# A two-layer hybrid decoder trunk: HGRN2 decay levels in pairs, rounded inner norms and full-width transposes

## The chip, the cores and the metric

The kernel runs on one core of one Trainium2 chip. The metric is the device time of one execution in microseconds. The engines are named as in the profile: PE (TensorE's products), PEld (TensorE's weight loads), DVE (VectorE), ACT (ScalarE), POOL (GpSimd) and SP (SyncE, which here issues weight loads from memory).

## The reference

One inference step of two layers, for a prompt of 256 tokens and 8 samples of 4 tokens each, with the same weights. The model is 1024 wide. A layer is

```
u    = RMSNorm(x)                      # x: 288 tokens x 1024
cols = u @ W_in                        # one projection, split among four mixers and four gate blocks
o_A  = RG-LRU(cols)    o_B = RWKV-7(cols)    o_C = HGRN2(cols)    o_D = dilated attention(cols)
x   += W_o( sum_n sigmoid(G_n) * (o_n @ P_n) )
v    = RMSNorm(x)
x   += W_down( gelu(causal_dwconv3(v @ W_gate)) * (v @ W_up) )
```

and a last RMSNorm follows the second layer. Each mixer is 256 wide. HGRN2 (four heads, a state of 128 x 64 each), in chunks of tokens, is

```
bcum = cumsum(log f) ;  dec[t,s] = exp(bcum[t] - bcum[s]) for s <= t
att  = sum_k q[t,k] k[s,k] dec[t,s,k]
o    = (q * exp(bcum)) @ S + att @ v
S    = S * exp(bcum_last) + (k * exp(bcum_last - bcum))^T v
```

RWKV-7 (four heads of 64) updates a state by S = S w + (S a) b^T + v k^T and reads it with r; its output is normalised by head, given a bonus from r, k and v, and gated. The outputs are y for both groups and the new states of every mixer.

## The kernel before

Everything is kept with features on partitions and the N = 288 token columns (256 of the prompt, then 32 of the samples) along the free axis. A weight block of 128 x 1024 in 32 bits is loaded by SP; `chunk` (L320) splits it into a high half, rounded to fp32r by ACT (L185, tile `h`), and a low half, the rest, by DVE (L193, tile `l`). Three buffers of each exist (TAGS, L135). `prod` (L330) then makes three products per 128 x 128 block: high by high, high by low, low by high, each with 288 columns. The tiles `tp` hold the halves of the normalised x, `pm` and `xc` are accumulators. There are 7,200 such products in the program; we call them projections. Three helpers record every product, transpose and activation, so all of these carry one line each: `mm` L179, `tr` L182, `act` L185; `tt` (L193), `stt` (L196) and `ts` (L200, L202) record element-wise work on DVE, or on POOL where the engine is given as G.

A product whose inputs are plain 32-bit tiles is done unrounded and leaves two records in the trace; one of fp32r tiles leaves one. `exact` (L357) splits a tile into rounded halves first and makes two rounded products. `square_sum` (L363) is the RMS norm's sum: POOL squares and adds seven of the eight blocks of x, ACT squares the eighth, and two unrounded products with a matrix of ones sum over partitions into `xc`; then ACT takes logarithm and exponential, which gives the row scale `rs`. It is called four times, and the first norm has a form of its own (`first_norm`, L389).

The mixers are Python generators: A (RG-LRU), B (RWKV-7), S (B's samples), C twice (HGRN2, one pass for each pair of heads), D (attention), E (its samples). `unit` writes three blocks of a projection and then calls `mix`, which takes up to four of the generators one step further, each up to its next `yield`; GAP and ORDER (L140, L147) set the pace. A scheduler then sets every engine's own order at build time with a timeline of its own, so a changed step moves its neighbours too. The accumulator banks limit how far steps can run ahead: three `pm`, two `xb` (RWKV, attention), three `xc` (HGRN2, the projections without mixers).

In `branch_c`, after the gates and a running sum b of log f, the scores of a chunk of 64 tokens are made by levels. Level m (1, 2, 4, 8, 16, 32) looks at blocks of 2m tokens: POOL subtracts from b its value at the block's middle (`tt(G, ...)`), ACT takes the exponentials of both halves, DVE multiplies the first half by k and the second by q (tiles `c`), PE makes eight 64 x 64 products (`level_out`), and a masked copy (`copy_predicated`, L971) puts those entries of the result that the level owns into the score tile `att` (`kc`). The diagonal is a level of its own, with k and q as they are. For the samples, whose chunks are four tokens, the diagonal and levels 1 and 2 also make two 32 x 32 products each, copied into `zs` (L977). Later steps transpose v and the decayed k with `tr`, or with products by an identity for the sample part, and multiply the samples' old state (`s0`) by q in one 32-row product for each head.

In `branch_b`, `scores` makes the products of two of the tiles at, rt, bt, kt, head by head, for 128-token chunks; three masked score matrices `zz` come from (kt, at), (bt, rt) and (kt, rt). The inner norms (`bones`, `cent`: block matrices of ones) go by `exact` with temporaries of the tag `b`, of which there are 20.

Of the kernel before, what the change touches and what calls it, by code (L numbers as in the profile page):

```python
# [18 lines left out]
P = 128  # L19
# [3 lines left out]
NB = 8  # L23
# [29 lines left out]
for _n, _c in CONSTS:  # L53
# [3 lines left out]
         ("b1", 32), ("l2", 32), ("l4", 32), ("l8", 32), ("l16", 32), ("dg", 64), ("us", 128), ("ui", 128),  # L57
# [7 lines left out]
def _constants():  # L65
# [40 lines left out]
    for w in (1, 2, 4, 8, 16, 32):  # L106
        def half(a, b):
            return (a // (2 * w) == b // (2 * w)) & (a % (2 * w) < w) & (b % (2 * w) >= w)
        putm(f"u{w}", half(s, t))
# [4 lines left out]
    putm("dg", s == t)  # L114
# [9 lines left out]
    putm("sdg", s == t)  # L124
    return {"cst": c, "msk": m, **{k: v.astype(np.float32) for k, v in more.items()}}


def dkeys():
# [7 lines left out]
        "tmp": (1152, 4), "rs": (1152, 1), "a": (1280, 10), "b": (1152, 20), "kb": (2048, 10), "c2": (2688, 10), "kc": (2048, 7),  # L136
# [14 lines left out]
def trunk(ctx, tc, I, O):  # L151
# [68 lines left out]
    V.memset(ones, 1.0)  # L220
    few = cp.tile([P, 4], F32, name="few")
# [141 lines left out]
    def square_sum():  # L363
# [4 lines left out]
        for k in range(KT):  # L368
            q = T("tmp")
            if k < KT - 1:  # L370
                tt(G, q, x[:, k], x[:, k], MUL)
                if acc is not None:
                    tt(G, q, q, acc, ADD)
                acc = q
            else:
                act(q, x[:, k], AF.Square)
            if k >= KT - 2:
                mm(p, ones, q, start=k == KT - 2, stop=k == KT - 1)
        r = T("rs")
# [141 lines left out]
    def branch_b(l, cols, rs, ys_, spawn):  # L521
# [25 lines left out]
        at, rt, bt, kt, bv, elast = [], [], [], [], [], []  # L547
# [4 lines left out]
        for i in range(2):  # L552
# [10 lines left out]
            lw, ta = T("b"), T("b")  # L563
# [7 lines left out]
        for i in range(2):  # L571
            pn = X("xb")[:, :N]
            exact(pn, bones, pre[i][3], "b")
# [6 lines left out]
        for i in range(2):  # L580
# [6 lines left out]
            b = T("b")  # L587
            stt(b, ta, 1.0, kk, ADD, MUL)

            ep, em = T("b"), T("b")  # L590
# [28 lines left out]
            exact(pb, bones, rk, "b")  # L619
# [129 lines left out]
        for pair in (((0, bt, 0), (0, kt, 1)), ((0, v, 2), (1, v, 2)), ((1, bt, 0), (1, kt, 1))):  # L749
# [24 lines left out]
        for m in (2, 4, 8, 16):  # L774
# [7 lines left out]
            V.transpose(fl(Y4), fl(X4))  # L782

# [29 lines left out]
        zz = [[], []]  # L813
        for a, q, mk in ((kt, at, "us"), (bt, rt, "ui"), (kt, rt, "ui")):
            pair = scores(a, q)
            yield
            for h, p in enumerate(pair):
                z = R([P, 4, P], "kb")
                G.memset(z, 0.0)
                V.copy_predicated(z, Mn(mk, 4), p)  # L820
                zz[h].append(z)
# [64 lines left out]
        for i in range(2):  # L886
            p = X("xb")[:, :N]
            exact(p, cent, py[i], "b")
# [5 lines left out]
        for i in range(2):  # L894
            p = X("xb")[:, :N]
            exact(p, bones, sqs[i], "b")
# [15 lines left out]
    def branch_c(l, i, cols, rs, ys):  # L912
# [690 lines left out]
```

## The time and profile before

| | |
|---|---|
| median of 3 runs | 1209.07 us (1206.88 to 1209.87) |
| profiled execution | 1212.02 us |
| its span, first to last instruction | 1210.2 us |
| mean granted clock of TensorE | 0.990 |
| busy: PE / PEld / DVE / ACT / POOL | 97% / 91% / 70% / 51% / 46% |
| read from memory, written | 187.08 MB, 6.49 MB |

Busy shares are means over the whole span; stretches differ, so the tables by stretch and the timelines matter more. A granted clock of 1.00 is 2.4 GHz, 0.50 is 1.2 GHz. In a timeline the bracket behind a row gives the idle time in front of that instruction on its engine and what released it. Matmuls are pipelined, so on PE the distance from one start to the next is the price of a product, and not its length.

### The profile page before, as it was taken

The numbers are of one execution on the slowest core, as the hardware profiler recorded it, in microseconds if no ns is written. First come the engines' busy times: TensorE is split into PE (matmuls) and PEld (weight loads), VectorE is DVE, ScalarE is ACT, GpSimd is POOL, SyncE is SP. The second block draws the span as 40 slices with busy tenths as digits, with TensorE's granted clock in tenths as the row PEclk, the third lists the DMA queues.
The fourth block names the chain that finished last, engine by engine and source line by source line (L and its number), as shares of the span: only waits on it lengthen the run. The fifth ranks groups of instructions, "written<-read, shape, count | busy, mean of one in ns | idle before, by whom it ended". The sixth has DMA issues, their size and how long they took to land.

```text
span 1210.2 us, 26415 instructions
## 1 busy us (share of the span) xinstructions
PE 1172.3 (97%) x10564; PEld 1102.2 (91%) x10564; DVE 848.4 (70%) x1385; ACT 611.3 (51%) x1042; POOL 552.8 (46%) x864
## 2 busy tenths in 40 slices
PE   7998999999999999999998999999999999999997
PEld 6987788998999999999998977899889999999996
DVE  7898856566578888865568888566655878888543
ACT  5776447445355444443367844565444554444332
POOL 3744555250345665642238337524221736665322
PEclk9999999999999999999998999999999999999999
DMA  7444145357645555454543432643775445545552
GB/s 258 132 130 141 63 152 203 112 168 277 209 133 190 161 171 168 164 176 163 171 153 124 141 106 89 214 145 115 253 250 168 150 152 171 172 158 171 167 171 77
DMA packets 64043, 196.33 MB, mean 162 GB/s; under 512 B 8417, under 2 KB 12641, under 8 KB 63921
## 3 DMA queue, kind: packets, MB, share of 16 engines
q1 hardware_dynamic: 61872, 189.56, 47.4%
q0 software_dynamic: 1328, 4.33, 1.0%
q8 instruction: 83, 1.36, 0.5%
q10 hardware_dynamic: 720, 0.76, 0.2%
q14 instruction: 40, 0.32, 0.1%
HBM read 187.08 MB, written 6.49 MB: 160 GB/s over the span
## 4 chain that ended last, share of the span: by engine, by line
PE 74%; DVE 9%; POOL 6%; ACT 4%; DMA 4%; issue 3%; DVEq 0%; SPq 0%; ACTq 0%; POOLq 0%
PE pm L179 43%; PE xc L179 24%; PE xb L179 5%; DVE c L193 2%; DVE l L193 2%; POOL b L193 1%; ACT L185 1%; DMA c<-in_vc 1%; DMA w<-in_w 1%; DVE b L196 1%; POOL a L193 1%; ACT a L185 1%; ACT h L185 1%; PE xc L182 1%; DMA kc<-in_cs 1%
## 5 line engine op out<-in xcount | busy, mean ns | idle before, releaser
L179 PE MATMUL pm<-tp,h 128*128 128x288 f32 x2880 | 608.3, 302 | 3.8 <-ACT h L185 2.3
L185 ACT ACTIVATE h<-w 128x1024 fp32r<-128x1024 f32 x299 | 316.5, 1059 | 393.8 <-issue 182.1
L179 PEld LDWEIGHTS pm<-tp,h 128*128 128x128 f32 x2880 | 471.3, 191 | 17.7 <-issue 7.3
L193 DVE TENSOR_TENSOR l<-w,h 128x1024 fp32r<-128x1024 f32 x299 | 380.6, 1273 | 118.6 <-ACT h L185 117.6
L179 PE MATMUL pm<-tp,l 128*128 128x288 f32 x1440 | 430.4, 299 | 4.5 <-DVE l L193 4.5
L179 PEld LDWEIGHTS pm<-tp,l 128*128 128x128 f32 x1440 | 274.7, 191 | 7.1 <-DVE l L193 5.0
L179 PE MATMUL xc<-tp,h 128*128 128x288 f32 x896 | 183.9, 296 | 1.6 <-ACT tp L185 0.9
L179 PEld LDWEIGHTS xc<-tp,h 128*128 128x128 f32 x896 | 144.7, 188 | 3.3 <-ACT tp L185 1.3
L179 PE MATMUL xc<-tp,l 128*128 128x288 f32 x448 | 132.3, 295 | 0.0
L193 POOL TENSOR_TENSOR tmp<-a,rs 128x256 f32<-128x256 f32 x96 | 73.5, 785 | 71.7 <-ACT a L185 71.7
L193 POOL TENSOR_TENSOR tp<-tp,th 128x288 f32<-128x288 f32 x48 | 52.3, 1111 | 109.3 <-DVE th L196 109.3
L196 DVE SCALAR_TENSOR_TENSOR a<-a,pv,a 128x304 f32<-128x304 f32 (+2 forms) x112 | 83.8, 749 | 11.2 <-ACT a L185 9.5
L179 PEld LDWEIGHTS xc<-tp,l 128*128 128x128 f32 x448 | 84.3, 188 | 0.4 <-DVE l L193 0.4
L193 POOL TENSOR_TENSOR tmp<-x 128x288 f32<-128x288 f32 x28 | 28.2, 1008 | 108.2 <-DVE x L193 107.9
L193 DVE TENSOR_TENSOR th<-pm,rs 128x288 f32<-128x288 f32 x64 | 29.1, 455 | 59.3 <-PE pm L179 59.2
L193 POOL TENSOR_TENSOR c<-c 128x512 f32<-128x512 f32 (+2 forms) x32 | 36.9, 1173 | 35.4 <-DVE kb L193 25.4
L193 DVE TENSOR_TENSOR tmp<-pm,tmp 128x288 f32<-128x288 f32 x48 | 22.0, 458 | 40.1 <-POOL tmp L193 40.1
L185 ACT ACT_TABLE_LOAD x34 | 43.6, 1283 | 0.6
L185 ACT ACTIVATE c<-c 128x256 f32<-128x256 f32 (+2 forms) x68 | 30.6, 500 | 20.9 <-POOL c L193 15.5
L185 ACT ACTIVATE a<-a 128x304 f32<-128x304 f32 (+2 forms) x76 | 33.6, 445 | 13.6 <-DVE a L196 7.8
L193 DVE TENSOR_TENSOR c<-c,c 128x256 f32<-128x256 f32 (+2 forms) x56 | 38.8, 734 | 1.7 <-ACT c L185 1.4
L179 PE MATMUL pm<-y,h 128*128 128x288 f32 x192 | 39.8, 299 | 0.0
(302 smaller groups left out, 1879.1 us busy)
## 6 DMA issues: line engine op xcount, KB each, us to landing
w<-in_wf SPq DMA_DIRECT2D x96, 512.0 KB, 3.5
w<-in_wg SPq DMA_DIRECT2D x64, 512.0 KB, 3.8
w<-in_w SPq DMA_DIRECT2D x59, 512.0 KB, 3.6
w<-in_wd SPq DMA_DIRECT2D x48, 512.0 KB, 3.5
c<-in_kc SPq DMA_DIRECT2D x32, 320.0 KB, 6.2
c<-in_vc SPq DMA_DIRECT2D x32, 320.0 KB, 5.3
w<-in_wb SPq DMA_DIRECT2D x16, 512.0 KB, 3.6
w<-in_wo SPq DMA_DIRECT2D x16, 512.0 KB, 3.5
```

Of the source, the lines that this page charges most:

```text
L179: return nc.tensor.matmul(o, a, b, start=start, stop=stop)
L182: nc.tensor.transpose(o, i, ident)
L185: S.activation(o, i, f, **kw)
L193: e.tensor_tensor(o, a, b, op)
L196: V.scalar_tensor_tensor(o, a, s, b, op0, op1)
```

## The change

HGRN2. `level_out` takes one or two levels and puts both into one accumulator, and the samples' products come as one 64 x 64 product for both heads. The diagonal's products go: level 1 now multiplies full tiles, exp(-d) by k and exp(d) by q, and its mask takes the diagonal along (u1 and s1d). Levels 4 and 8, and 16 and 32, go out in pairs, so the products of 4 (and of 16) wait for the factors of 8 (and of 32). The masked copies of a pair, and the samples' two, follow it. The samples' state product takes the q of both heads (64 columns), with one 32-row multiplication by the mask for each head behind it.

Norms. The three calls of `square_sum` ahead of the last add the eighth square on POOL too and then go by `exact` with a rounded matrix of ones; the last call keeps the old form.

RWKV. at and rt lie side by side in one tile `ar` (two buffers), and kt is multiplied by both in one product of 256 columns. The zeroed score tiles are made ahead; the transposes of v move behind the first inversion, those of bt and kt between the score steps. The inner norms' temporaries take the tag `yb`, b reuses ta, and the tag `b` has 16 buffers in place of 20; in the feed-forward part two of the `b` pairs take `ar` instead.

Transposes of 32 or 64 columns take 128 columns that end at the same place, in HGRN2 and in the attention, and the copies behind them read from the partitions where the wanted part then lies.

How this stands in the engines' orders, at three places. TensorE, layer one, where HGRN2's levels (`xc<-c`, 64x64; 32x32 the samples' part) run among projections (`pm<-tp,h`, `pm<-tp,l`) and RWKV's steps (`xb`); before:

```order
L179 MATMUL xc_1953<-c_179 64x64 x5
L179 MATMUL xb_1220<-b_1091,zs 32x64 x4
L179 MATMUL xc_1953<-c_179 64x64 x3
L179 MATMUL pm_1965<-tp_95,l_1969 128x288
L179 MATMUL xc_2000<-c_178 64x64 x8
L179 MATMUL xc_2010<-c_179 32x32 x2
L179 MATMUL pm_1965<-tp_97,h_1968 128x288
L179 MATMUL pm_1965<-tp_98,h_1968 128x288
L179 MATMUL pm_1965<-tp_97,l_1969 128x288
L179 MATMUL pm_1965<-tp_99,h_1968 128x288
L182 MATMUL xb_1229<-cst,b_973 128x128 x2
```

In the order before, one level fills a tile with 8 products, the samples' two have a tile of their own, and projections stand between. The same place after:

```order
L179 MATMUL xb_1197<-kb_1193,ar_799 32x512 x2
L179 MATMUL xb_1197<-kb_1194,ar_840 32x512 x2
L179 MATMUL xb_1204<-kb_1202,b_1121 32x32 x32
L179 MATMUL xc_1994<-c_1988 64x64 x9
L179 MATMUL xc_2018<-c_181 64x64 x8
L179 MATMUL xc_2018<-c_2012 64x64
L179 MATMUL xb_1247<-kb_1193,ar_799 32x512 x2
L179 MATMUL xb_1247<-kb_1194,ar_840 32x512 x2
L179 MATMUL xb_1272<-b_1089,zs 32x64 x4
L179 MATMUL xc_2018<-c_2012 64x64 x7
L179 MATMUL xc_2078<-c_180 64x64 x8
L179 MATMUL pm_2038<-tp_102,h_2041 128x288
```

Eight products of a level with one of its samples share a tile (`xc_1994`), two levels share the next one (`xc_2018`, from `c_181` and `c_2012`), and RWKV's sample, state and inversion products stand between them.

VectorE, layer two, from a low half of weights (`l`) on: factors of the levels (`c<-c,c`), masked copies into `kc` and `zs`; before:

```order
L193 TENSOR_TENSOR l_9864<-w_9861,h_9863 128x1024
L971 COPY_PREDICATED kc_9418<-msk,xc_9563 128x256
L977 COPY_PREDICATED zs<-msk,xc_9573 64x32
L977 COPY_PREDICATED zs<-msk,xc_9596 64x32
L193 TENSOR_TENSOR c_9655<-c_9655,c_9286 128x32x8
L193 TENSOR_TENSOR c_9655<-c_9655,c_8732 128x32x8
L971 COPY_PREDICATED kc_9386<-msk,xc_9605 128x256
L971 COPY_PREDICATED kc_9418<-msk,xc_9645 128x256
L971 COPY_PREDICATED kc_9386<-msk,xc_9661 128x256
L193 TENSOR_TENSOR c_9677<-c_9677,c_9192 128x32x8
L193 TENSOR_TENSOR c_9677<-c_9677,c_8381 128x32x8
L193 TENSOR_TENSOR c_7728<-c_7728,c_9286 128x16x16
```

Each level's copy stands in front of the next factors. After, where L995 and L998 are the masked copies and L787 is RWKV's:

```order
L193 TENSOR_TENSOR l_9897<-w_9894,h_9896 128x1024
L193 TENSOR_TENSOR c_9476<-c_9476,c_9281 128x32x8
L193 TENSOR_TENSOR c_9476<-c_9476,c_8778 128x32x8
L995 COPY_PREDICATED kc_9406<-msk,xc_9458 128x256
L998 COPY_PREDICATED zs<-msk,xc_9458 32x32 x2
L193 TENSOR_TENSOR c_9536<-c_9536,c_9198 128x32x8
L787 COPY_PREDICATED b_8586<-msk,xb_8825 128x256
L193 TENSOR_TENSOR c_9536<-c_9536,c_8351 128x32x8
L788 STREAM_TRANSPOSE b_8585<-b_8586 128x256
L193 TENSOR_TENSOR c_7698<-c_7698,c_9281 128x16x16
L193 TENSOR_TENSOR kb_8657<-xb_8876,kb_8657 128x512
L193 TENSOR_TENSOR c_7698<-c_7698,c_8778 128x16x16
```

The factors of levels 8 and 16 stand ahead of the paired copies, and RWKV's copies stand between them.

ScalarE at the boundary of the layers, from the table load on, with the square `tmp`, the roundings `h` of two weight blocks, and the row scale `rs`; before:

```order
L189 ACT_TABLE_LOAD
L185 ACTIVATE tmp_7694<-x 128x288
L185 ACTIVATE h_7815<-w_7813 128x1024
L185 ACTIVATE rs_7697<-xc_7671,few 128x288
L185 ACTIVATE h_7853<-w_7851 128x1024
L185 ACTIVATE rs_7697<-rs_7697 128x288
```

After:

```order
L189 ACT_TABLE_LOAD
L185 ACTIVATE tmp_7658<-x 128x288
L185 ACTIVATE tmp_7661<-tmp_7658 128x288
L185 ACTIVATE h_7785<-w_7783 128x1024
L185 ACTIVATE h_7823<-w_7821 128x1024
L185 ACTIVATE rs_7667<-xc_7636,few 128x288
L185 ACTIVATE rs_7667<-rs_7667 128x288
```

The square is followed by its own high half, and both roundings stand ahead of the logarithm.

The diff, cut to what changes the work ("..." marks what is left out):

```diff
@@ -54,7 +54,7 @@
     COFF[_n] = NCST
     NCST += _c
 MASKS = [("u1", 64), ("u2", 64), ("u4", 64), ("u8", 64), ("u16", 64), ("u32", 64),
-         ("b1", 32), ("l2", 32), ("l4", 32), ("l8", 32), ("l16", 32), ("dg", 64), ("us", 128), ("ui", 128),
+         ("b1", 32), ("l2", 32), ("l4", 32), ("l8", 32), ("l16", 32), ("s1d", 32), ("us", 128), ("ui", 128),
...
+        putm(f"u{w}", half(s, t) | (s == t) if w == 1 else half(s, t))
         if f"l{w}" in MOFF:
...
-    putm("dg", s == t)
...
+    putm("s1d", (s // 2 == t // 2) & (s <= t))
...
 TAGS = {"w": (4096, 3), "h": (4096, 3), "l": (4096, 3), "th": (1152, 8), "tp": (1152, 24), "y": (1152, 5), "yb": (1152, 4),
-        "tmp": (1152, 4), "rs": (1152, 1), "a": (1280, 10), "b": (1152, 20), "kb": (2048, 10), "c2": (2688, 10), "kc": (2048, 7),
+        "tmp": (1152, 4), "rs": (1152, 1), "a": (1280, 10), "b": (1152, 16), "ar": (2304, 2), "kb": (2048, 10), "c2": (2688, 10), "kc": (2048, 7),
         "sm": (512, 8)}
...
+    rones = cp.tile([P, P], F32R, name="rones")
+    V.tensor_copy(rones, ones)
...
-    def square_sum():
+    def square_sum(last=False):
         p = X("xc")[:, :N]
         acc = None
@@ -369,13 +371,15 @@
             q = T("tmp")
             if k < KT - 1:
                 tt(G, q, x[:, k], x[:, k], MUL)
-                if acc is not None:
-                    tt(G, q, q, acc, ADD)
-                acc = q
             else:
                 act(q, x[:, k], AF.Square)
-            if k >= KT - 2:
+            if acc is not None and (k < KT - 1 or not last):
+                tt(G, q, q, acc, ADD)
+            acc = q
+            if last and k >= KT - 2:
                 mm(p, ones, q, start=k == KT - 2, stop=k == KT - 1)
+        if not last:
+            exact(p, rones, acc, "tmp")
         r = T("rs")
...
+            ar.append(R([P, 2, N], "ar"))
+            lw, ta = ar[i][:, 0], T("b")
...
-            exact(pn, bones, pre[i][3], "b")
+            exact(pn, bones, pre[i][3], "yb")
...
-            b = T("b")
+            b = ta
 
-            ep, em = T("b"), T("b")
...
-        for pair in (((0, bt, 0), (0, kt, 1)), ((0, v, 2), (1, v, 2)), ((1, bt, 0), (1, kt, 1))):
+
+        def token_major(*pair):
...
+        yield from token_major((0, v, 2), (1, v, 2))
...
-        zz = [[], []]
-        for a, q, mk in ((kt, at, "us"), (bt, rt, "ui"), (kt, rt, "ui")):
-            pair = scores(a, q)
+        zz = [[R([P, 4, P], "kb") for _ in range(3)] for _ in range(2)]
+        for z in zz[0] + zz[1]:
+            G.memset(z, 0.0)
+        for i in range(2):
+
+            pair = [X("xb"), X("xb")]
+            for c in range(2):
+                s = slice(c * P, c * P + P)
+                for h in range(2):
+                    mm(pair[h][:, c * TP:(c + 1) * TP], kt[i][rows(h), s], ar[i][rows(h), :, s])
             yield
             for h, p in enumerate(pair):
-                z = R([P, 4, P], "kb")
-                G.memset(z, 0.0)
-                V.copy_predicated(z, Mn(mk, 4), p)
-                zz[h].append(z)
+                p = p.rearrange("p (c a b) -> p c a b", c=2, a=2)
+                for m, mk in ((0, "us"), (2, "ui")):
+                    V.copy_predicated(zz[h][m][:, 2 * i:2 * i + 2], Mn(mk, 2), p[:, :, m // 2])
+        yield from token_major((0, bt, 0), (0, kt, 1))
+        pair = scores(bt, rt)
+        yield
+        for h, p in enumerate(pair):
+            V.copy_predicated(zz[h][1], Mn("ui", 4), p)
+        yield from token_major((1, bt, 0), (1, kt, 1))
...
-        def level_out(sk, sq, mask, smask):
+        def level_out(*levels):
+
             p = X("xc")
-            for c in range(2):
-                for h in range(2):
-                    z = 2 * c + h
-                    for r in range(2):
-                        cs = slice(h * TP + c * P + 64 * r, h * TP + c * P + 64 * r + 64)
-                        mm(p[rows(r), z * 64:z * 64 + 64], sk[:, cs], sq[:, cs])
-            yield
-            V.copy_predicated(att, Mn(mask, 4), p[:, :256].rearrange("p (a b) -> p a b", a=4))
-            if smask is not None:
-                p = X("xc")
-                for h in range(2):
-                    mm(p[hr(h), :NS], sa(sk, h), sa(sq, h))
-                yield
-                V.copy_predicated(zi, M(smask)[0:64], p[0:64, :NS])
-        yield from level_out(k, q, "dg", "sdg")
+            for n, (sk, sq, _, smask) in enumerate(levels):
+                for c in range(2):
+                    for h in range(2):
+                        z = 4 * n + 2 * c + h
+                        for r in range(2):
+                            cs = slice(h * TP + c * P + 64 * r, h * TP + c * P + 64 * r + 64)
+                            mm(p[rows(r), z * 64:z * 64 + 64], sk[:, cs], sq[:, cs])
+                if smask is not None:
+                    mm(p[0:64, 256:320], sk[:, PW:], sq[:, PW:])
+            yield
+            for n, (_, _, mask, smask) in enumerate(levels):
+                V.copy_predicated(att, Mn(mask, 4), p[:, n * 256:(n + 1) * 256].rearrange("p (a b) -> p a b", a=4))
+                if smask is not None:
+                    for h in range(2):
+                        V.copy_predicated(zi[hr(h)], M(smask)[hr(h)], p[hr(h), 256 + NS * h:256 + NS * (h + 1)])
+
...
+            if m == 1:
+                d2 = T("c2", W2)
+                act(d2, d, AF.Exp)
+                act(d, d, AF.Exp, scale=-1.0)
+                tt(V, d, d, k, MUL)
+                tt(V, d2, d2, q, MUL)
+                yield from level_out((d, d2, "u1", "s1d"))
+                continue
             lo, hi = bl(d)[:, :, :m], bl(d)[:, :, m:]
             act(lo, lo, AF.Exp, scale=-1.0)
             act(hi, hi, AF.Exp)
             tt(V, lo, lo, bl(k)[:, :, :m], MUL)
             tt(V, hi, hi, bl(q)[:, :, m:], MUL)
-            yield from level_out(d, d, f"u{m}", f"s{m}" if m <= 2 else None)
+            level = (d, d, f"u{m}", f"s{m}" if m == 2 else None)
+            if m in (4, 16):
+                first = level
+                continue
+            yield from level_out(*([level] if m == 2 else [first, level]))
 
...
-        for c in range(2):
-            tr(p[:, c * P:(c + 1) * P], v[:, c * P:(c + 1) * P])
-        for h in range(2):
-            mm(p[hr(h), 256:320], v[rows(h), TP:N], ident[rows(h), rows(h)])
+
+        for c in range(3):
...
-        act(vt[0:64, 256:], p[0:64, 256:320], AF.Copy)
+        for h in range(2):
+            act(vt[hr(h), 256:], p[96:128, 256 + 64 * h:320 + 64 * h], AF.Copy)
...
-            mm(p[hr(h)], sa(qh, h), s0[h].rearrange("p b v -> p (b v)"))
+            mm(p[rows(h)], qh[:, PW:], s0[h].rearrange("p b v -> p (b v)"))
-        tt(V, own[0:64], p[0:64].rearrange("p (b v) -> p b v", b=NB), bc(C("vexp")[0:64], 2, [64, NB, 64]), MUL)
+        for h in range(2):
+            r = slice(96 * h, 96 * h + 32)
+            tt(V, own[hr(h)], p[r].rearrange("p (b v) -> p b v", b=NB), bc(C("vexp")[r], 2, [NS, NB, 64]), MUL)
         V.tensor_reduce(so[0:64], own[0:64].rearrange("p b v -> p v b"), AX.X, ADD)
...
-        tr(p[0:64, :P], kh[:, PW:])
+        tr(p[:, :P], kh[:, W2 - P:])
...
-            act(kst[0:32, h], p[hr(h), :P], AF.Copy)
-            act(kst[32:64, h], p[hr(h), :P], AF.Copy)
-            tt(V, kst[64:96, h], p[hr(h), :P], kst[0:32, h], SUB)
+            r = slice(64 + NS * h, 64 + NS * (h + 1))
+            act(kst[0:32, h], p[r, :P], AF.Copy)
+            act(kst[32:64, h], p[r, :P], AF.Copy)
+            tt(V, kst[64:96, h], p[r, :P], kst[0:32, h], SUB)
...
-            if n < 10:
+            if n < 8:
...
-                t = R([P, 2, N], "c2", F32R)
+                t = R([P, 2, N], "ar" if n < 10 else "c2", F32R)
...
-    rs = square_sum()
+    rs = square_sum(True)
```

## Rows read from the trace of the kernel before

**Rows 1.** The page, part 1: busy microseconds of each engine, share of the span, instructions.
```profile
PE 1172.3 (97%) x10564; PEld 1102.2 (91%) x10564; DVE 848.4 (70%) x1385; ACT 611.3 (51%) x1042; POOL 552.8 (46%) x864
```

**Rows 2.** TensorE timeline, levels: start, length, engine, line, operation, tiles, shapes, records.
```profile
129.92 0.29 PE L179 MATMUL pm<-tp,l 128*128 128x288 f32 x1
130.15 0.31 PE L179 MATMUL xb<-sm,sm 32*32 32x64 f32 x8
130.39 1.34 PE L179 MATMUL xc<-c 128*64 128x64 f32 x36
131.66 0.53 PE L179 MATMUL pm<-tp,h 128*128 128x288 f32 x2
132.03 0.29 PE L179 MATMUL pm<-tp,l 128*128 128x288 f32 x1
132.16 0.29 PE L179 MATMUL pm<-tp,h 128*128 128x288 f32 x1
```

**Rows 3.** TensorE timeline at the layer boundary, a product with ones.
```profile
606.66 0.65 PE L179 MATMUL xc<-tmp,ones 128*128 128x288 f32 x2
606.93 0.63 PE L179 MATMUL pm<-tp,h 128*128 128x288 f32 x2
607.40 0.29 PE L179 MATMUL pm<-tp,l 128*128 128x288 f32 x1
```

**Rows 4.** Groups by form, TensorE: busy us, mean ns, idle before and releaser.
```profile
L179 PE MATMUL xb<-b,b 64*128 64x128 f32 x128 | 16.6, 286 | 2.0 <-DVE kb L820 2.0
...
L179 PE MATMUL xc<-kc,kc 64*128 64x256 f32 x16 | 3.8, 390 | 0.0
...
L179 PE MATMUL xc<-c 128*32 128x32 f32 x32 | 2.0, 206 | 0.0
```

**Rows 5.** Busy us by stretch: TensorE, weight loads, VectorE, ScalarE, GpSimd; clock, DMA.
```profile
100.00:115.00 15.00, 11.93 (x93) 10.87 (x91) 15.00 (x34) 8.76 (x21) 9.18 (x9) 0.89 0.26 84
...
140.00:155.00 15.00, 12.86 (x197) 9.51 (x196) 15.00 (x23) 7.55 (x15) 9.27 (x14) 1.00 0.18 56
...
734.00:749.00 15.00, 12.86 (x197) 9.58 (x197) 15.00 (x23) 7.55 (x15) 9.28 (x14) 1.00 0.16 55
```

**Rows 6.** TensorE timeline at three waits: in brackets idle us and releaser.
```profile
69.01 0.40 PE L179 MATMUL xb<-b,blk 128*128 128x288 f32 x1 [2.77 <-ACT b L185]
...
109.72 0.40 PE L179 MATMUL pm<-tp,l 128*128 128x288 f32 x1 [2.14 <-DVE l L193]
...
657.65 0.85 PE L179 MATMUL xb<-b,kb 64*128 64x288 f32 x1 [3.40 <-ACT b L185]
```

**Rows 7.** Groups by form, VectorE: HGRN2 products, masked copies, state product.
```profile
L193 DVE TENSOR_TENSOR c<-c,c 128x256 f32<-128x256 f32 x32 | 25.4, 832 | 1.7 <-ACT c L185 1.4
...
L971 DVE COPY_PREDICATED kc<-msk,xc 128x256 f32<-128x256 uint8 x28 | 12.3, 440 | 3.4 <-PE xc L179 3.2
...
L193 DVE TENSOR_TENSOR c<-c,c 128x576 f32<-128x576 f32 x8 | 7.2, 915 | 0.0
...
L193 DVE TENSOR_TENSOR c<-c,c 128x288 f32<-128x288 f32 x16 | 6.2, 450 | 0.0
...
L193 DVE TENSOR_TENSOR c<-xc,cst 64x512 f32<-64x512 f32 x4 | 2.7, 681 | 7.6 <-PE xc L179 7.6
```

**Rows 8.** VectorE timeline in the level stretch, two places.
```profile
129.38 0.41 DVE L193 TENSOR_TENSOR c<-c,c 128x256 f32<-128x256 f32 x1
...
138.42 4.46 DVE L193 TENSOR_TENSOR c<-c,c 128x256 f32<-128x256 f32 x4
```

**Rows 9.** GpSimd timeline beside the second of them.
```profile
138.94 3.66 POOL L193 TENSOR_TENSOR c<-c 128x512 f32<-128x512 f32 x3
```

**Rows 10.** ScalarE timeline at the layer boundary: square, first weight rounding, exponential.
```profile
609.52 0.45 ACT L185 ACTIVATE tmp<-x 128x288 f32<-128x288 f32 x1
612.53 1.06 ACT L185 ACTIVATE h<-w 128x1024 fp32r<-128x1024 f32 x1 [2.56 <-issue]
...
615.04 0.42 ACT L185 ACTIVATE rs<-rs 128x288 f32<-128x288 f32 x1
```

More of the change, by code (lines that the diff above doesn't have):

```diff
@@ L108, in half @@
             return (a // (2 * w) == b // (2 * w)) & (a % (2 * w) < w) & (b % (2 * w) >= w)
-        putm(f"u{w}", half(s, t))
+        putm(f"u{w}", half(s, t) | (s == t) if w == 1 else half(s, t))
         if f"l{w}" in MOFF:
@@ L546, in branch_b @@
         r, k, v, wa, gl = [cm[0], cm[1]], [cm[2], cm[3]], [cm[4], cm[5]], cm[6], cm[7]
-        at, rt, bt, kt, bv, elast = [], [], [], [], [], []
+        ar, at, rt, bt, kt, bv = [], [], [], [], [], []
         lm = T("sm", 8)
@@ L562, in branch_b @@
             yield
-            lw, ta = T("b"), T("b")
+            ar.append(R([P, 2, N], "ar"))
+            lw, ta = ar[i][:, 0], T("b")
             act(lw, pw, AF.Tanh, scale=0.5, bias=dcol(l, "hw0", i))
@@ L586, in branch_b @@
             tt(G, k2, k2, k[i], MUL)
-            b = T("b")
+            b = ta
             stt(b, ta, 1.0, kk, ADD, MUL)
-            ep, em = T("b"), T("b")
+            ep, em = ar[i][:, 1], T("b")
             for c in range(3):
@@ L618, in branch_b @@
             pb = X("xb")[:, :N]
-            exact(pb, bones, rk, "b")
+            exact(pb, bones, rk, "yb")
             yield
@@ L887, in branch_b @@
             p = X("xb")[:, :N]
-            exact(p, cent, py[i], "b")
+            exact(p, cent, py[i], "yb")
             yield
@@ L895, in branch_b @@
             p = X("xb")[:, :N]
-            exact(p, bones, sqs[i], "b")
+            exact(p, bones, sqs[i], "yb")
             yield
@@ L1039, in branch_c @@
         p = X("xc")
-        for c in range(2):
-            tr(p[:, c * P:(c + 1) * P], v[:, c * P:(c + 1) * P])
-        for h in range(2):
-            mm(p[hr(h), 256:320], v[rows(h), TP:N], ident[rows(h), rows(h)])
+        for c in range(3):
+            o = min(c * P, N - P)
+            tr(p[:, c * P:(c + 1) * P], v[:, o:o + P])
         yield
@@ L1199, in branch_d @@
         for c in range(3):
-            w = P if c < 2 else NS
+            o = min(c * P, N - P)
             p = X("xc")
             for i in range(2):
-                tr(p[:w, i * P:(i + 1) * P], v[i][:, c * P:c * P + w])
+                tr(p[:, i * P:(i + 1) * P], v[i][:, o:o + P])
             yield
             t = T("a", 256)
-            act(t[:w], p[:w, :256], AF.Copy)
+            if c < 2:
+                act(t, p[:, :256], AF.Copy)
+            else:
+                act(t[:NS], p[96:128, :256], AF.Copy)
             vt.append(t)
@@ L1249, in samples @@
             tr(p[:, 0:P], e[:, 512:640])
-            tr(p[:NS, P:2 * P], e[:, 640:672])
+            tr(p[:, P:2 * P], e[:, 544:672])
             yield
             act(pt[:, 4], p[:, 0:P], AF.Copy)
-            act(ptn[:NS], p[:NS, P:2 * P], AF.Copy)
+            act(ptn[:NS], p[96:128, P:2 * P], AF.Copy)
             po = X("xb")
```

## The prediction

> **What bounds the kernel now.** I read the page first [rows 1]: TensorE has work on it for 97% of the span, VectorE for 70%. So the count of TensorE's products sets the time, except where another engine makes TensorE wait. Then TensorE's timeline, for the price of a product [rows 2]: the big projections (128x288, rounded fp32r) start 0.13 us apart (132.03 to 132.16), and 7,200 of them are the bulk of the program. A small product in a row of its like is cheap: 36 records (an unrounded product is two) start between 130.39 and 131.66, 0.07 us a product. But where the tile shape changes the step is longer: the 128x288 product at 129.92 is followed at 130.15 by 32x32 tiles, 0.23 us instead of 0.13. So each change of tile shape costs about 0.10 us.
>
> Then a table by stretch [rows 5]. Between 100 and 115 us and between 140 and 155 us VectorE is busy all the time (15.00 of 15.00) and TensorE is not (11.93 and 12.86); 734 to 749 in layer two repeats it. These two stretches are where HGRN2 starts and where its decay levels run; here VectorE leads. Last, the longest single waits [rows 6]: 2.77 us at 69.01 and 3.40 us at 657.65, both on ScalarE in front of an RWKV product, and 2.14 us at 109.72 on VectorE's low halves of weights. A long wait costs twice: in 100 to 115 us the mean granted clock is 0.89, that is, some 3.3 us at 1.2 instead of 2.4 GHz, about 1.7 us of lost work.
>
> **The change, part by part, on TensorE.**
>
> Sample scores and the diagonal level. Each of four HGRN2 passes (two layers, two head pairs) drops the diagonal's eight 64x64 products, which now come out of level 1, and six 32-wide sample products; it gains two 64-wide sample products. Over the program that is 24 products of 64x64 and 24 of 32x32 less. At 0.07 us [rows 2] the first are 1.7 us. The second are at most 0.125 us (2.0 us busy for 16 products, rows 4), which still holds the pipeline's tail; I take 0.06, near the 64-wide ones, so 1.4 us (bounds 0 and 3.0).
>
> Changes of tile shape. In TensorE's order I count 318 places before where a product's tile shape differs from the last one's, and 261 after: two levels share one run, and sample products now have the prompt products' shape. 57 x 0.10 us = 5.7 us. This is the largest term. Bounds: 0, if such a gap is hidden wherever TensorE waits anyway, and 5.7.
>
> Inner norms. Three of the five sums of squares used two unrounded products with the ones matrix; they now use a rounded one on a high and a low half. The old product: from 606.66 to 607.40 there are it and two projections, 0.74 - 2 x 0.13 = 0.47 us [rows 3]. The new one is 0.13. 6 x 0.34 = 2.0 us. The last norm, on the kernel's tail, keeps the old form, so the tail does not move.
>
> RWKV scores. 32 products of 128 columns become 16 of 256. A pair of the first is 2 x 0.26 us (16.6 us busy for 64), one of the second form 0.475 (3.8 us for 8) [rows 4]: 16 x 0.045 = 0.7 us.
>
> 128-column transposes: ten-odd cheap small pieces become full ones of the same length. Zero, within 0.5 us either way.
>
> Sum on TensorE: 1.7 + 1.4 + 5.7 + 2.0 + 0.7 = 11.5 us.
>
> **On the other engines.** Level 1 now needs two full products of 128x576 (0.915 us each) where two halves of 128x288 (0.450) did, and saves one masked copy (0.440) [rows 7]: 2 x 0.465 - 0.44 = +0.5 us of VectorE a pass. The pass lies in a stretch that VectorE leads, so I put all four on the path: +2.0 us. Splitting the state's sample product into two 32-row ones adds 0.68 us a pass [rows 7], after the levels, where TensorE has projections to do: zero. The extra adds, copies and low halves of the norms lengthen the chain to the row scale: the square is done at 609.97, and before, the scale is done at 615.46, with two weight roundings in between on ScalarE [rows 10]. After, ScalarE's order puts the high half and both roundings ahead of the logarithm, so the chain gets a GpSimd add and two copies (about 2 us) into a gap that was idle from 609.97 on: zero; if not, the fourth projection of layer two waits up to 2 us for a bank. RWKV's fewer buffers: its temporaries are also fewer, zero.
>
> What the new order does to the waits. The products of levels 4 to 32 stood among 29 projections in each layer; now they stand among 25 in layer one and 9 in layer two. VectorE has there, in layer two, a run of 30 instructions between two roundings of weights where it had 16. TensorE, which runs in order, stands at a level's products until VectorE has made both factors. VectorE's work for all this is the same as before, so the waits of 2.1 us in each such stretch stay, I think, at their sum. RWKV's normalisation gets its rounding on ScalarE right behind its squares, which should shorten the waits at 69.01 and 657.65, while its second pair follows one projection behind the first and not six, which lengthens them again. I count zero, with 5 us either way.
>
> Here one thing speaks against the change. Four level products in a row took 4.46 us, 1.1 us each, while GpSimd was subtracting (3.66 us for three); one of the same size with no subtraction beside it took 0.41 [rows 8, 9]. The Trainium skill (GPSIMD Engine Reference, 1. Specifications) says that GpSimd shares its SBUF interfaces with VectorE and contends with VectorE's instructions that read two SBUF inputs. The trace agrees: 1.1 against 0.41 us.
>
> Net: 11.5 - 2.0 = 9.5 us less. The profiled execution took 1212.02 us (span 1210.2), so 1202.5 for one like it; the median of the runs is 1209.07, 3 us lower, so 1199.6. I say 1200.
>
> **The rivals.**
>
> The gain drowns in VectorE's pace. Where VectorE is busy throughout, a shorter product only makes TensorE wait longer. For it: 15.00 of 15.00 in two stretches of each layer [rows 5]. Against: only some 30 us a layer are like that, and the shape changes go in the RWKV stretches too. If levels and half the shape changes are lost (3.1 + 2.9), 9.5 shrinks to 3.5: 1205.6. With one more wait, no change.
>
> The packed levels choke (slower). Place: HGRN2's levels, on VectorE. Its 32 level products average 0.832 us [rows 7], a mix of 0.41 and over 1.1. If packing puts all of them beside a subtraction, that is 32 x (1.1 - 0.83) = 8.6 us; the sixteen 128x576 products of the levels' ends and starts, longer in the same ratio (a third), add 5 us. Two waits over 2 us a layer more would cost 1.7 us of clock each, once or twice: 3 us. 1200 + 16.6 = 1216. It decides from the point where more than about 20 of the 32 products run beside a subtraction. Against: GpSimd's subtractions are no more than before, and VectorE finishes them earlier.
>
> The waits go. If the RWKV waits (2.8 and 3.4 us) and the clock behind them (1.7 and 3.4) mostly vanish because RWKV now runs some 40 projections earlier, another 8 to 10 us: 1191.
>
> That the change does not do what it says: TensorE's order shows the merged runs, so only their price is open.
>
> **How the numbers follow.** The forecast has 0.50 (1195 to 1205), the waits going 0.17 (to 1188), the gain drowned 0.18 (1205 to 1212), the choke 0.15 (1213 and up). Measured against the median, 0.3% is 3.6 us, about what a measurement of this kernel can tell: faster is below 1205.4, slower above 1212.7. Faster 0.50 + 0.17 + 0.02 of the drowned = 0.69; no change 0.17; slower 0.14. The range takes the waits going and the drowned gain in, and cuts into the choke: 1188 to 1213.
>
> **What would show it.** TensorE's levels should have fewer, longer runs, and TensorE's idle time in the HGRN2 start and level stretches should stay near 3 and 2 us with VectorE at full. The norm's ones products should be single 0.13 us steps. If the mean of the 128x256 level products rises from 0.83 to 1.1 us, the choke is right; if the waits before the RWKV normalisation fall under 1 us and the clock stays at 1.00 there, the gain is larger. The forecast is wrong if the sum of TensorE's waits in either layer changes by more than 5 us.

## The result

The changed kernel took 1220.59 us (median of 4 runs, 1218.62 to 1221.87) against 1209.47 for the one before (4 runs, 1206.88 to 1212.2): ratio 1.0086, interval 1.0062 to 1.0111. It is slower by some 11 us; 9.5 less were forecast. The profiled execution took 1220.68 us, span 1218.9, clock 0.987.

The page after, part 1, as in [rows 1]:

```profile
PE 1167.3 (96%) x10418; PEld 1094.9 (90%) x10418; DVE 847.8 (70%) x1401; ACT 620.4 (51%) x1053; POOL 545.6 (45%) x867
```

Three numbers of a page split the span. Span less PE busy is TensorE's idle time: 37.9 us before, 51.6 after. Span x (1 - clock) is work lost to the half clock: 12.1 and 15.8 (some 2 us of either at the end of the span, where TensorE has nothing left to do). PE busy less that is TensorE's own work at full clock: 1160.2 and 1151.5. So own work fell by 8.7 us, idle time rose by 13.7 and lost clock by 3.7: together the 8.7 us between the spans. The listed clocks of all runs say the same more strongly: lost clock is 10.0 us on average over the 69 runs of before in this study, and 16.1 over the four of after.

Where it sits: the tables by stretch, cut at the same VectorE instructions in both kernels (mixers of layer one, norm ahead of its feed-forward part, feed-forward part and boundary, then layer two). Columns: the stretch, its length, busy us of PE, PEld, DVE, ACT, POOL, granted clock, DMA share, GB/s. Before:

```profile
18.47:358.64 340.17, 329.88 (x3377) 296.94 (x3376) 238.28 (x438) 186.70 (x361) 148.77 (x223) 0.98 0.48 160
358.64:387.68 29.04, 28.76 (x212) 28.09 (x211) 23.09 (x30) 16.46 (x23) 15.46 (x14) 1.00 0.48 162
387.68:617.31 229.63, 229.63 (x1734) 229.42 (x1733) 164.80 (x231) 102.72 (x136) 110.05 (x188) 1.00 0.52 169
617.31:951.18 333.87, 324.04 (x3338) 291.31 (x3337) 232.48 (x405) 182.43 (x355) 146.72 (x220) 0.98 0.48 158
951.18:980.18 29.00, 28.71 (x212) 28.23 (x211) 22.86 (x30) 16.54 (x23) 15.80 (x17) 1.00 0.49 162
```

After:

```profile
18.51:359.04 340.53, 324.14 (x3308) 290.71 (x3307) 236.61 (x444) 190.53 (x366) 146.54 (x223) 0.99 0.49 159
359.04:389.69 30.65, 28.80 (x212) 27.93 (x211) 23.39 (x31) 16.95 (x24) 16.43 (x16) 1.00 0.52 156
389.69:618.34 228.65, 228.65 (x1729) 228.56 (x1728) 165.11 (x232) 101.85 (x135) 106.94 (x189) 1.00 0.55 168
618.34:957.29 338.95, 324.26 (x3268) 290.53 (x3268) 231.74 (x412) 187.82 (x361) 143.32 (x220) 0.97 0.49 157
957.29:989.68 32.39, 30.45 (x212) 29.57 (x211) 23.47 (x31) 16.87 (x24) 16.66 (x18) 0.95 0.49 148
```

The mixers of layer one end level (+0.4): TensorE is busy 5.7 us less there and idle 6.1 us more (16.39 us of idle time for 10.29). Those of layer two lose 5.1, with 4.9 us more idle time. The two norms ahead of the feed-forward parts lose 1.6 and 3.4 us, the second with a clock of 0.95. The boundary norm gives 1.0 back.

The waits of the mixers in TensorE's timeline after (in brackets idle us and releaser), against [rows 6] ("..." marks rows left out):

```profile
69.00 0.53 PE L179 MATMUL xb<-yb,blk 128*128 128x288 f32 x2 [1.80 <-ACT ar L185]
74.21 0.40 PE L179 MATMUL pm<-tp,l 128*128 128x288 f32 x1 [0.72 <-DVE l L193]
77.63 0.40 PE L179 MATMUL xb<-yb,blk 128*128 128x288 f32 x1 [0.75 <-ACT yb L185]
81.10 0.40 PE L179 MATMUL xb<-yb,blk 128*128 128x288 f32 x1 [0.95 <-ACT yb L185]
...
109.52 0.77 PE L179 MATMUL xc<-c,c 128*64 128x64 f32 x18 [0.92 <-DVE c L193]
...
120.84 0.77 PE L179 MATMUL xc<-c 128*64 128x64 f32 x18 [2.49 <-DVE c L193]
...
703.07 0.50 PE L179 MATMUL pm<-tp,h 128*128 128x288 f32 x2 [1.48 <-DVE a L193]
705.50 0.48 PE L179 MATMUL pm<-tp,l 128*128 128x288 f32 x1 [1.94 <-DVE l L193]
```

The wait of 2.77 us at RWKV's first norm shrank to 1.80, but three of 0.7 to 0.95 stand behind it. At 120.84 level 2 (eight products and one of the samples, 18 records) waits 2.49 us for its factors, right behind RWKV's products.

The groups that answer to [rows 4, 7], RWKV's scores and HGRN2's factors, after:

```profile
L179 PE MATMUL xb<-ar,b 64*128 64x256 f32 x32 | 9.0, 402 | 0.0
L179 PE MATMUL xb<-ar,b 64*128 64x128 f32 x64 | 8.9, 291 | 0.0
```

```profile
L193 DVE TENSOR_TENSOR c<-c,c 128x256 f32<-128x256 f32 x32 | 22.0, 712 | 0.9 <-ACT c L185 0.8
```

VectorE's 128x256 factor products fell from 832 to 712 ns on average. How TensorE starts RWKV's scores, eight products of 128 columns before (16 records), then two of 256 after (4 records), each with the row behind:

```profile
199.45 1.71 PE L179 MATMUL xb<-b,b 64*128 64x128 f32 x16
201.09 0.67 PE L179 MATMUL xc<-a,blk 128*128 128x288 f32 x3
```

```profile
178.29 1.13 PE L179 MATMUL xb<-ar,b 64*128 64x256 f32 x4
179.35 0.24 PE L179 MATMUL xc<-cst,sm 32*64 32x32 f32 x1
```

### The profile page after: what moved, and what is told of

It is laid out like the page before. It is cut to its first block, busy times and chain, and to the rows that moved or that the text cites. A ratio compares the mean times of both kernels' runs of the same rounds, so it can differ in the third digit from the quotient of the medians.

```text
span 1218.9 us, 26143 instructions
## 1 busy us (share of the span) xinstructions
PE 1167.3 (96%) x10418; PEld 1094.9 (90%) x10418; DVE 847.8 (70%) x1401; ACT 620.4 (51%) x1053; POOL 545.6 (45%) x867
## 5 line engine op out<-in xcount | busy, mean ns | idle before, releaser
L179 PEld LDWEIGHTS pm<-tp,l 128*128 128x128 f32 x1440 | 274.9, 191 | 11.5 <-DVE l L193 5.5
L193 POOL TENSOR_TENSOR tmp<-tmp,tmp 128x288 f32<-128x288 f32 x27 | 35.3, 1306 | 13.6 <-ACT tmp L185 11.7
```

Of the source, the lines that this page charges most:

```text
L179: return nc.tensor.matmul(o, a, b, start=start, stop=stop)
L193: e.tensor_tensor(o, a, b, op)
```

## The experiments

The changed kernel has four parts; each was put alone into the kernel before, then cut further. "Work", "idle" and "lost" are the three terms above, of one profiled execution against that of before. Single executions of one kernel differ by some us in these terms, so the last column gives means over all runs of a kernel against the 69 of before (1198.7 and 10.0 us): the span without lost clock ("rest", work and idle time together), and lost clock.

| kernel | median us | ratio (interval) | work, idle, lost | means: rest, lost |
|---|---|---|---|---|
| after | 1220.59 | 1.0086 (1.0062 to 1.0111) | -8.7, +13.7, +3.7 | +3.7, +6.2 |
| norms alone | 1214.07 | 1.0036 (1.0025 to 1.0047) | -3.2, +2.4, +4.9 | 0.0, +4.1 |
| norms, sum in xb | 1208.88 | 0.9984 (0.9969 to 0.9998) | -3.7, +0.6, 0.0 | -4.0, +2.4 |
| levels alone | 1200.02 | 0.9918 (0.9903 to 0.9933) | -8.7, -0.8, -2.5 | -12.2, +2.0 |
| levels, unpaired | 1204.66 | 0.9955 (0.994 to 0.997) | -9.1, -0.8, +6.0 | -12.1, +6.9 |
| RWKV alone | 1223.65 | 1.0108 (1.009 to 1.0125) | +1.7, +9.2, +5.1 | +9.2, +4.5 |
| RWKV without yb | 1217.63 | 1.0053 (1.0034 to 1.0073) | +3.2, +4.4, -2.4 | +7.1, +0.2 |
| RWKV without the move | 1216.88 | 1.0055 (1.0035 to 1.0074) | +3.9, +4.2, -3.6 | +8.2, -0.9 |
| RWKV without both | 1216.84 | 1.0053 (1.0035 to 1.0071) | +0.5, +1.1, +1.2 | +3.8, +2.4 |
| RWKV buffers alone | 1219.2 | 1.0072 (1.0047 to 1.0097) | -2.1, +8.0, +1.3 | +4.6, +3.6 |
| wide alone | 1216.55 | 1.0051 (1.0034 to 1.0068) | +1.0, +2.1, +3.7 | +2.0, +3.7 |
| wide, transposes alone | 1215.5 | 1.0048 (1.003 to 1.0067) | +1.6, +3.8, -2.4 | +3.8, +2.2 |
| after, sum in xb | 1216.19 | 1.0044 (1.0028 to 1.006) | -9.5, +13.7, +3.7 | -0.8, +6.2 |
| levels and norms, sum in xb | 1197.07 | 0.9887 (0.9865 to 0.9908) | -10.1, +0.1, -4.9 | -12.2, -0.8 |
| after without RWKV, sum in xb | 1197.37 | 0.9896 (0.9877 to 0.9915) | -12.0, +2.0, -4.9 | -11.8, -1.4 |

The medians of before beside them were 1210.15 to 1210.94 (1209.47 beside the changed kernel). The four parts alone make +3.7, -10.4, +13.3 and +6.2 us, together +12.8, where the whole change made +11.1. They don't simply add, though: by the last three rows the wide part costs nothing beside the levels, and RWKV's costs some 18 us there, where it costs 13 alone.

**Norms alone** (the sums of squares of the RMS norms).

```diff
-                mm(p, ones, q, start=k == KT - 2, stop=k == KT - 1)
+        if not last:
+            exact(p, rones, acc, "tmp")
```

> The kernel before with the norm part alone (rounded ones product, eighth square added on GpSimd). Theory: in the trace after, the two norms ahead of the feed-forward part cost 1.6 and 3.2 us, because TensorE's order there puts a whole projection ahead and then stands 0.4 and 1.2 us at the last block and at a weight rounding; the norm at the layer boundary gives 0.7 back and the tail 0.4. TensorE's order at these norms is the same with this part alone, so it should cost about 3.7 us: 1213 us. Rival: the loss there comes from what the mixers leave behind, and the part alone brings its forecast 2 us: 1207.

1214.07: close to the theory's 1213. The same waits stand in this trace and in that of after; in after, TensorE (columns as above) and ScalarE at layer one's norm:

```profile
380.59 0.40 PE L179 MATMUL pm<-tp,h 128*128 128x288 f32 x1 [0.39 <-DVE tp L196]
380.83 0.29 PE L179 MATMUL pm<-tp,l 128*128 128x288 f32 x1
382.30 0.53 PE L179 MATMUL pm<-tp,h 128*128 128x288 f32 x2 [1.18 <-ACT h L185]
382.76 0.40 PE L179 MATMUL xc<-tmp,rones 128*128 128x288 f32 x1
```

```profile
379.56 1.28 ACT L189 ACT_TABLE_LOAD   x1
380.85 0.44 ACT L185 ACTIVATE tmp<-x 128x288 f32<-128x288 f32 x1
381.20 1.04 ACT L185 ACTIVATE h<-w 128x1024 fp32r<-128x1024 f32 x1
```

TensorE has finished one projection up to the last block of x, waits for it, and the next one's weights are rounded only behind the table load and the square.

**Norms, the sum in another bank.**

```diff
-        p = X("xc")[:, :N]
+        p = X("xc" if last else "xb")[:, :N]
```

> The norm part alone as before, but the sum of squares goes into one of RWKV's two accumulators (xb), which are idle at the norms, in place of one of HGRN2's three (xc). Same arithmetic, same chain to the row scale. Theory: the 3.7 us that the part cost come from the order, not from the longer chain: with the bank out of the projections' way, TensorE's order again has two projections side by side at the norm, the waits there (1.9 and 2.0 us in the part's trace, 0.3 each before) and the half clock behind the second go, and the rounded products keep their 3 us: 1207. Rival: the row scale simply comes 2 us later and the wait stays: 1214.

1208.88: the theory holds, 1.9 us above its number; by the interval the gain over before is 0.2 to 3.8 us. In TensorE's order the first gate projection stood behind the first ones product while the sum held an xc bank; with xb two projections run side by side there as before. At layer one's norm TensorE has no gap in this trace (16.00 of 16.00), and the ones products lie between projections:

```profile
374.00:390.00 16.00, 16.00 (x123) 16.00 (x122) 12.62 (x21) 9.66 (x14) 6.38 (x13) 1.00 0.55 173
```

```profile
382.92 0.29 PE L179 MATMUL xb<-tmp,rones 128*128 128x288 f32 x1
...
383.46 0.29 PE L179 MATMUL xb<-tmp,rones 128*128 128x288 f32 x1
```

**Levels alone.**

```diff
-        yield from level_out(k, q, "dg", "sdg")
+                yield from level_out((d, d2, "u1", "s1d"))
+            yield from level_out(*([level] if m == 2 else [first, level]))
```

> The kernel before with the HGRN2 level part alone (pairs of levels, diagonal in level 1, shared sample scores). Theory: TensorE's own work falls by some 5 us over both layers, VectorE's extra multiplications and the waits for both factors of a pair give 3 to 5 us of it back: 1207 to 1210. Rival: the levels bring their forecast gain when RWKV doesn't move beside them: 1203 to 1205. Second rival: they are the main cost, by waits for factors: over 1214.

1200.02: better than the theory and than its first rival. Work fell by 8.7 us where the theory had 5, and idle time did not rise: VectorE's dearer level 1 does not show in it.

**Levels without pairs.**

```diff
-            if m in (4, 16):
-                first = level
-                continue
-            yield from level_out(*([level] if m == 2 else [first, level]))
+            yield from level_out(level)
```

> The level part with every level in an accumulator of its own, as before (no pairs of levels); diagonal in level 1 and shared sample scores stay. Theory: the gain of 10 us is TensorE's own work (9 us less in the trace), of which the pairs, two in each of four passes, have only some 1.6 us of changes of shape: 1202 to 1203. Rival: the pairs are the gain: 1206 and more. Second rival: waiting for both factors of a pair costs, and single levels are faster: under 1199.

1204.66: between the theory's range and the first rival's, in neither. Own work is the same with and without pairs (-9.1, -8.7). The pairs save 10 changes of tile shape (310 in this trace, 300 with pairs), at 0.10 us each 1.0 us, which is too little to tell in these terms. What the pairs bring is clock: lost clock is 16.8 us on average over the runs without them, 12.0 with, and the rest is the same.

**RWKV alone.**

```diff
+            ar.append(R([P, 2, N], "ar"))
-            exact(pn, bones, pre[i][3], "b")
+            exact(pn, bones, pre[i][3], "yb")
+        yield from token_major((0, v, 2), (1, v, 2))
```

> The kernel before with the RWKV part alone (at and rt side by side, fewer b buffers, inner norms by the yb tag, transposes moved). Theory: the 256-column score products cost 0.5 us a layer more than two of 128 in the trace after (4.23 against 3.71 us for the same scores), and the new waits at RWKV's norms (three of 0.7 to 1.0 us in layer one at 74 to 81 us, 2 to 3 us a layer behind its end) outweigh what it saves at 69 us: 1213 to 1216. Rival: the waits belong to HGRN2's run that shares VectorE, and the part alone changes nothing: 1208 to 1210.

1223.65: well above the theory's range, the costliest part. In layer two TensorE stands twice where HGRN2 starts:

```profile
709.88 0.50 PE L179 MATMUL pm<-tp,h 128*128 128x288 f32 x2 [2.41 <-ACT c L185]
...
712.85 0.61 PE L179 MATMUL pm<-tp,l 128*128 128x288 f32 x1 [1.53 <-DVE l L193]
```

**RWKV, temporaries in b again,** and **RWKV, transposes at their old place.**

```diff
-            exact(pn, bones, pre[i][3], "yb")
+            exact(pn, bones, pre[i][3], "b")
```

> The RWKV part alone, with the inner norms' temporaries back in the tag b (16 buffers) instead of yb. Theory A: yb's four buffers tie each norm to the one before it, and the waits in front of the norms (0.7, 0.9 us at 79 and 82 us, 0.6 at 225, 1.2 to 1.5 behind) are their price; without it the part costs half: 1216. Theory B: the cost is in the earlier chain (the transposes moved), which this kernel keeps: 1222 to 1224.

```diff
+        for pair in (((0, bt, 0), (0, kt, 1)), ((0, v, 2), (1, v, 2)), ((1, bt, 0), (1, kt, 1))):
+            yield from token_major(*pair)
-        yield from token_major((0, v, 2), (1, v, 2))
```

> The RWKV part alone, with the transposes of v, bt and kt back at their old place ahead of the inversion. In TensorE's order the inversion and the state steps then stand about as late as before (1026 projections into the layer's count where it was 1044, and 913 with the move). Theory B: moved, the chain lies in the stretch that VectorE leads for HGRN2's levels, and the waits at 149 to 154 us and behind the gates at 241 to 247 us (1.4, 0.8, 0.8 and 1.2, 1.5 us) are its price: without the move 1214 to 1216. Theory A: the buffers are the cost, and it stays at 1222 to 1224.

1217.63 and 1216.88: each edit, taken out, gives 6 to 7 us back, so neither theory alone is right.

**RWKV without both.**

```diff
-            exact(pn, bones, pre[i][3], "yb")
-        yield from token_major((0, v, 2), (1, v, 2))
```

> The RWKV part without the yb temporaries and without the moved transposes: only at and rt side by side, the 256-column products and 16 b buffers are left. Theory: the two edits taken out cost 6.0 and 6.8 us and add up to nearly the whole 13.2: 1210 to 1212, with the 256-column products 0.5 us a layer dearer than two of 128. Rival: the two overlap (either alone lets the chain wait), and 1214 to 1216 is left.

1216.84: in the time no better than with one of them, as the rival has it (0.8 us above its range); some 6 us are left. The means part it: the rest falls from +9.2 to +7.1 and +8.2 with one edit out and to +3.8 with both, and lost clock is lower with one out (+0.2, -0.9) than with both out (+2.4). What each edit alone gave back was mostly clock.

**RWKV, the buffers alone.** The tile `ar`, b in ta's place and 16 b buffers, with the old scores:

```diff
-        zz = [[R([P, 4, P], "kb") for _ in range(3)] for _ in range(2)]
+        for a, q, mk in ((kt, at, "us"), (bt, rt, "ui"), (kt, rt, "ui")):
+            pair = scores(a, q)
```

> The RWKV part's buffers alone: at and rt in the tile ar, b in ta's place, 16 b buffers; the scores stay six sets of 128-column products with their old masked copies and transposes. Theory: the 6.2 us that were left with the 256-column products are the buffers' (the first weight waits of 1.3 us at 86 us and the later norms come from an order with fewer b's): 1215 to 1217. Rival: the 256-column products and their half-width masked copies are the price: 1210 to 1212.

1219.2: the buffers, above the theory's range; the 256-column products are not the price of the 6 us. Which of the three (the tile `ar`, b in ta's place, 16 buffers for 20) costs it is open. TensorE's timeline of this kernel, layer one:

```profile
87.42 0.40 PE L179 MATMUL pm<-tp,l 128*128 128x288 f32 x1 [1.25 <-DVE l L193]
...
105.65 0.43 PE L179 MATMUL xb<-cst,b 64*32 64x64 f32 x16 [1.67 <-ACT kb L185]
```

How the buffers make VectorE's low half late at 87.42 is not shown.

**Wide alone,** and **the wide transposes alone.**

```diff
-            mm(p[hr(h)], sa(qh, h), s0[h].rearrange("p b v -> p (b v)"))
+            mm(p[rows(h)], qh[:, PW:], s0[h].rearrange("p b v -> p (b v)"))
-        tr(p[0:64, :P], kh[:, PW:])
+        tr(p[:, :P], kh[:, W2 - P:])
```

> The kernel before with the 128-column transposes and the samples' state product of both heads alone. Theory: the same number of products with fewer changes of tile shape, 1207 to 1209. Rival: the split multiplication behind the state product (0.69 us twice instead of once) comes on the path: 1211.

```diff
-            mm(p[rows(h)], qh[:, PW:], s0[h].rearrange("p b v -> p (b v)"))
+            mm(p[hr(h)], sa(qh, h), s0[h].rearrange("p b v -> p (b v)"))
```

> The 128-column transposes alone, the samples' state product as before. Theory: the part's 6 us came from one wait of 1.8 us at 872 us in front of a transpose in the attention and the half clock behind it, which the state product's two split multiplications on VectorE push there; without them 1209 to 1211. Rival: the transposes and the copies from the upper partitions cost by themselves: 1214 to 1217.

1216.55 and 1215.5: both theories missed, and the state product is not the cause; the rival of the second run has its number (1214 to 1217). In the wide part's trace one wait in the attention is followed by half clock:

```profile
872.32 0.30 PE L182 MATMUL xc<-cst,kc 128*128 128x128 f32 x1 [1.83 <-DVE kc L200]
```

```profile
860.00:880.00 20.00, 18.17 (x121) 12.01 (x119) 9.31 (x23) 7.57 (x19) 0.00 (x0) 0.85 0.89 316
```

With the transposes alone the wait at this place is longer, and the clock stays up:

```profile
873.07 0.30 PE L182 MATMUL xc<-cst,kc 128*128 128x128 f32 x1 [2.05 <-DVE kc L200]
```

```profile
860.00:880.00 20.00, 17.95 (x143) 12.41 (x143) 10.04 (x25) 7.95 (x21) 0.00 (x0) 1.00 0.85 295
```

This wait and its like in layer one (1.48 us at 277.57) are 3.5 of the 3.8 us of idle time that this trace has more than before, where TensorE has no gap in either place. The levels' trace has nearly the same wait, also without half clock:

```profile
858.32 0.30 PE L182 MATMUL xc<-cst,kc 128*128 128x128 f32 x1 [1.65 <-DVE kc L200]
```

```profile
845.00:865.00 20.00, 18.35 (x146) 12.97 (x144) 10.22 (x25) 8.35 (x23) 0.00 (x0) 1.00 0.83 277
```

**After with the other bank,** and **after without the RWKV part, with the other bank.** The first is the one-line edit of the bank above, the second takes the RWKV part out as well.

```diff
-        p = X("xc")[:, :N]
+        p = X("xc" if last else "xb")[:, :N]
```

> The changed kernel with only the bank of the norms' sums changed (xb for xc). Theory: the norms' 5.2 us between the two banks (1214.1 and 1208.9 alone) carry over: 1215 to 1216 where the changed kernel took 1220.6. Rival: beside the RWKV part's order the waits at the norms come back elsewhere: 1219 to 1221.

> Levels, norms with the other bank, and wide transposes; only the RWKV part left out of the changed kernel. Theory: the wide part's 5 to 6 us came mostly from a wait in front of one attention transpose (1.5 us at 278 us, 2.0 us at 873 us), and the level part's trace has that wait already (1.2 and 1.6 us), so here it adds little: 1198 to 1200. Rival: the parts add up: 1202 to 1203.

1216.19: the 4.4 us of the bank carry over. The waits at the two norms are gone from this trace; its profiled execution (1219.9 us) is the second longest of twelve, with longer waits elsewhere, so the gain shows in the means (rest -0.8 for +3.7) and not in the three terms. 1197.37: without RWKV's part the wide part costs nothing beside the levels. That its 5 to 6 us alone come from the waits in the attention is made likely by this, not shown.

**Levels and norms, sum in xb.** Both diffs above, without the RWKV and wide parts.

> The level part and the norm part with the other bank, no RWKV part and no wide transposes. Theory: the parts add up: 1200 less 3 us: 1197. Rival: the norm part costs its 3.7 us here too: 1204.

1197.07: the parts add up. This version beats the kernel before by 13.9 us (1210.94 beside it) and the changed one by some 23; the one without the RWKV part is level with it.

## Why the prediction was wrong

**The sum on TensorE was about right.** 11.5 us less were forecast, 8.7 measured. Not all of "work" is the work of the products that changed: by the distances from start to start in the traces, at full clock, the 7,200 projections, the same in every kernel, take 982 to 991 us (986 before); why is open. By the same distances the products into `xc` in tiles of 128x64 and 128x32, most of them HGRN2's, take 6.0 us less with the levels alone; the prediction's 1.7 + 1.4 us, and 3.0 for the 30 changes of tile shape that this trace has fewer (330 before, 300), make 6.1. So its largest term, 0.10 us for a change of shape, fits there, though no run tests it by itself: between single and paired levels 10 changes are too few to tell. The Trainium skill (TensorEngine Tiling (Array Packing), Key Properties) says that changing the tiling mode drains TensorE; the rows agree that such a step is longer (0.23 against 0.13, [rows 2]). The norms brought 3.2 to 3.7 us where 2.0 were put down.

The term for RWKV's scores had the wrong sign: [rows 4] give 16.6 us for 64 products of 128 columns, so 8.3 for the 32 that went; the 16 of 256 take 9.0. The price of 0.475 us came from another group (`xc<-kc,kc`). In the timelines eight products of 128 columns take 1.64 us before (199.45 to 201.09), and two of 256, the work of four, 1.06 us after (178.29 to 179.35), so the work of those eight now takes two short runs and 2.1 us.

**The step that failed** is the price of the new order: "so the waits of 2.1 us in each such stretch stay, I think, at their sum", with "I count zero, with 5 us either way" for RWKV, and zero for its buffers. Idle time rose by 13.7 us, by 6.1 in the mixers of layer one, past the 5 us that the prediction named as its sign of being wrong. With the levels alone the first of these holds (idle time -0.8). RWKV's zero fails: its part alone brings +9.2 us of idle time, and leaving it out of the changed kernel (sum in xb) takes idle time from +13.7 to +2.0 and the time from 1216.19 to 1197.37 us. Its buffers and the two other edits (yb, the moved transposes) share in it. By the releasers of its waits (ACT yb, ACT ar, DVE l) an early chain asks ScalarE and VectorE for results while both also serve HGRN2 and the weights. That reading is argued from the rows; the runs show only the sizes. It was seen in the order, that RWKV ran some 40 projections earlier, and read as a possible gain ("The waits go").

**The norms** were counted at -2.0 with a chain that hides. The chain did hide; what cost was the order around it, an accumulator bank held by the sum while the projections wanted it. The same edit with another bank gives the 2 us.

**The clock** was counted only as part of single waits. On average over the runs it is 6 us of the whole loss, more than half. In the norms part alone it is all of it (lost clock 14.1 against 10.0 us on average, the rest of the span 1198.7 in both): the waits there take what the products save. With the sum in xb the rest is 1194.7 and lost clock 12.4.

**The choke** was the right sign by the wrong mechanism, so its nearness to the measured time is luck: it needed level products of 1.1 us on VectorE, and they fell to 712 ns. **The extra 2.0 us of VectorE** in level 1 are not to be found in the idle time of the levels alone.

## What to carry to other kernels

When TensorE is busy 97% of the time and runs in order, price a change by what it does to three terms: its own work, its idle time, and the clock lost behind it; the first is easy to count and the other two decide. Try an edit's parts one by one: here one worth 10 us and one costing 13 came in the same diff. Try them together too, since what a part costs alone can vanish or grow beside another. Where a program orders the instructions, a held bank or a changed set of buffers can cost more than the products that the edit saves, and the fix can be one word. One profiled execution shows where the waits are; for how much is lost take the means of several runs.

## What was not expected of the hardware

Waits of the same kind, place and nearly the same length are followed by half clock in one execution and not in another (1.83 us with a granted clock of 0.85 in the 20 us around it, 2.05 us with 1.00), so lost clock varies by kernel and run: in the wide transposes' eight runs the listed clock goes from 0.987 to 0.996 and the time from 1220.22 to 1212.67. And an unrounded product of 256 columns with 64 rows was no cheaper than two of 128: 9.0 us of busy time for 16 against 8.9 for 32 in the same trace.
